# A hybrid attention layer on one core: the first weights on ScalarE's queue, the last product's last step in column halves, and a block of each last row on GpSimd

## The chip, the cores and the metric

The kernel runs on one core of a Trainium2 chip. The metric is the device time of one execution in microseconds (us); the lower the better. A core has five engines, each with its own instruction stream: TensorE (PE in the profile; PEld is its weight load), VectorE (DVE), ScalarE (ACT), GpSimd (POOL) and SyncE (SP). Here SyncE only issues transfers. A transfer can also be issued by ScalarE or GpSimd; the issue then stands in that engine's stream. The engines wait for each other by semaphores. TensorE writes to PSUM, whose banks hold 512 float32 columns on each of 128 partitions; VectorE and ScalarE read PSUM, GpSimd does not here.

## The reference, cut to what matters

One encoder layer over 16 meta tokens and 512 real tokens of width 2048:

```python
hn = rmsnorm(h, pre_norm_g[layer])
proj = jnp.einsum('bld,dc->blc', hn, w_in[layer])
qa, ka, va, ga, qb, kb, vb, gb = jnp.split(proj, SPLIT_POINTS, axis=-1)
ya = gqa_axial_mixer(qa, ka, va, ...) * jax.nn.silu(ga)
yb = diff_attn_mixer(qb, kb, vb, ...) * jax.nn.silu(gb)
y = jnp.einsum('blc,cd->bld', jnp.concatenate([ya, yb], axis=-1), w_out[layer])
h = h + rmsnorm(y, post_norm_g[layer])
return h[:, N_META:, :]
```

For this text two places matter: the first product (`hn` times the first columns of `w_in`) and the very last steps (`y`, its norm over the 2048 columns of each token, the gain, the residual).

## The kernel before, in words

Every float32 operand is split into two parts of a reduced float32 format, a high part (`wh`, `xh`, `t4h`: a copy on ScalarE) and a low part (`wl`, `xl`, `t4l`: the difference, on VectorE), and each product is three matmuls: high times high, low times high, high times low (`three`, and in `product` the three `mm` of `step`).

**The start.** SyncE's queue brings, in program order (`load` pins each transfer behind what was traced on its engine before), the tokens `xs` (one of 16 slices of 128 input columns by 528 tokens each) and the weights `st` (for two slices, 768 columns). ScalarE issues only `gcol`, the gain column, and then runs a small activation `warm`, ahead of which its function table is loaded. `xload(k)` scales a token slice by the gain into `xh[k]` (ScalarE, L191) and `xl[k]` (VectorE, L192). `wload` brings weights and splits them by `wsplit` (L156, L157); the first weights come in two parts of 384 columns, the first for slice 0, the second for slice 1. Meanwhile TensorE runs 16 matmuls on zeros (`heat`, into `hot`). Then the first product runs over the slices k: for each, three groups of columns (a group of keys in two halves of 264 tokens, two groups of 512 tokens), three matmuls each.

The middle (projections, two kinds of attention, the gates) isn't touched.

**The end.** The output projection is made of four blocks of 512 columns and four rows of 128 tokens (`y[t][g]`), by sums of blocks that need fewer products. The last call of `product` makes the last block (g = 2) of rows 0 and 1 (u = 0, 1): its first step i = 0 runs for both rows, then the last three steps first for row 0, followed by `done(0, ...)`, and then for row 1, followed by `done(1, ...)`. Here `done` is `end`. For its row it subtracts the product in PSUM from the block (VectorE, L1173), squares and sums it (ScalarE, L1082), takes the root with the partial sum of the other three blocks, `sspart` (ScalarE, L1162), multiplies by the gain `gpB` (VectorE, L1085), takes the reciprocal (VectorE, L1178), and then for each of the four blocks `row_block` (VectorE, L1167) scales by the row's factor `ry`, adds the residual `xres`, and has SyncE store 128x512 to the output. `order` (the same as `keep_in_program_order`) pins each of these behind the instruction traced before it on its engine. `GS = (0, 3, 1, 2)` is the order of the blocks. Row 0's fourth block is put behind row 1's subtraction. `part` (POOL, L1109 and L1111) makes `sspart` earlier.

What is not pinned is ordered by a scheduler with priorities; `lanes` interleaves the matmuls of attention with the rest by estimated times.

Of the kernel before, what the change touches and what calls it, by code (L numbers as in the profile page):

```python
# [10 lines left out]
F32 = mybir.dt.float32  # L11
F32R = mybir.dt.float32r
F16 = mybir.dt.float16
AF = mybir.ActivationFunctionType
ALU = mybir.AluOpType
AX = mybir.AxisListType

P = 128
DM = 2048
KT = DM // P  # L20
SEQ = 512
NM = 16
NT = SEQ + NM
TT = SEQ // P
HALF = NT // 2
# [16 lines left out]
class Lanes:  # L42
# [13 lines left out]
    def mm(self, out, lhsT, rhs, start, stop, **kw):  # L56
        n = int(np.prod(rhs.shape[1:]))
        us = max(n, 256) / 2370.0
        if rhs.dtype == F32:
            us = 4 * max(n, 128) / 2370.0  # L60
        self._add(self.nc.tensor.matmul(out, lhsT, rhs, start=start, stop=stop, **kw), us)  # L61
# [45 lines left out]
def kernel(ctx: ExitStack, tc: tile.TileContext, xT, xn, xm, w_s, w_t, w_q, w_o,  # L107
                             gpre, gq, gk, lams, gsub, gpost, ident_d, cos_d, sin_d, dist_d, out):
    nc = tc.nc
    lanes = Lanes(tc)  # L110
    mm, transpose = lanes.mm, lanes.transpose
# [4 lines left out]
    wp = ctx.enter_context(tc.tile_pool(name="wp", bufs=3))  # L116
# [12 lines left out]
    def ctile(shape, name, dt=F32, src=None, pool=cst):  # L129
        t = pool.tile(shape, dt, name=name, tag=name, bufs=1)  # L130
        if src is not None:
            load(t, src)
        return t
# [5 lines left out]
    def load(out, in_):  # L139

        tc.keep_in_program_order(nc.sync.dma_start(out=out, in_=in_))


    def wload(src, n=1024, dma=nc.sync.dma_start, parts=1):
        st = wp.tile([P, 1024], F32, name="st", tag="st")
        ws = None
        for i in range(parts):
            c = slice(i * n // parts, (i + 1) * n // parts)
            dma(out=st[:, c], in_=src if parts == 1 else src[:, c])
            ws = wsplit(st, c, ws)  # L150
        return ws

    def wsplit(st, c=slice(0, 1024), ws=None):
        wh, wl = ws or [wp.tile([P, 1024], F32R, name=n, tag=n) for n in ("wh", "wl")]
        with tc.high_priority(rank[0]):
            splits.append((nc.scalar.activation(wh[:, c], st[:, c], AF.Copy),  # L156
                           nc.vector.tensor_tensor(out=wl[:, c], in0=st[:, c],  # L157
                                                   in1=wh[:, c].bitcast(F32), op=ALU.subtract)))
        return wh, wl

    splits = []
# [3 lines left out]
    epst = ctile([P, 1], "epst")  # L165
    nc.vector.memset(epst, EPS)
    warm = ctile([P, 1], "warm")
    nc.scalar.activation(warm, epst, AF.Identity)

    heat = ap.tile([P, 256], F32R, name="heat", tag="pm", bufs=1)  # L170
    nc.vector.memset(heat.bitcast(F32), 0.0)
# [1 line left out]
    hot = pd.tile([P, 512], F32, name="hot", tag="pd")  # L173
    for i in range(16):
        mm(hot[:, :256], heat[:, :P], heat, start=True, stop=True)
    gcol = ctile([P, KT], "gcol")
    nc.scalar.dma_start(out=gcol, in_=gpre)

    def xtile(name, n, dt=F32R):

        return xp.tile([P, 576], dt, name=name, tag=f"x{n}")

    xh, xl = [[xtile(f"x{n}{k}", 2 * k + j)[:, :NT] for k in range(KT)]
              for j, n in enumerate("hl")]
    pad(xp, "xpad", 32)

    def xload(k):
        tag, n = ("p", 4) if k % 6 < 4 else ("tT", 2)
        st = ap.tile([P, NT], F32, name="xs", tag=tag, bufs=n)
        load(st, xT[k])  # L190
        nc.scalar.activation(xh[k], st, AF.Identity, scale=gcol[:, k:k + 1])  # L191
        nc.vector.scalar_tensor_tensor(out=xl[k], in0=st, scalar=gcol[:, k:k + 1],  # L192
                                       in1=xh[k].bitcast(F32), op0=ALU.mult, op1=ALU.subtract)

    KEYS = [(0, HALF), (HALF, NT)]
    REAL = [(NM, NT)]
# [1 line left out]
    def three(ps, wh, wl, k, n0, n1):  # L198
        mm(ps, wh, xh[k][:, n0:n1], start=(k == 0), stop=False)
        mm(ps, wh, xl[k][:, n0:n1], start=False, stop=False)  # L200
        mm(ps, wl, xh[k][:, n0:n1], start=False, stop=(k == KT - 1))
# [40 lines left out]
    start = [KEYS, REAL, REAL]  # L242
    first = [[pd.tile([P, 512], F32, name="pd", tag="pd") for _ in segs] for segs in start]
    for k0 in range(0, KT, 2):
        xload(k0)
        wh, wl = wload(w_s[k0 // 2], 768, load, 2 if k0 == 0 else 1)
        xload(k0 + 1)
        for k in (k0, k0 + 1):
            for i, (segs, pss) in enumerate(zip(start, first)):
                c = slice((i + 3 * (k - k0)) * P, (i + 3 * (k - k0) + 1) * P)  # L250
                for (n0, n1), ps in zip(segs, pss):
                    three(ps[:, :n1 - n0], wh[:, c], wl[:, c], k, n0, n1)
# [22 lines left out]
    for t in (TT, 0, 1, 2, 3):  # L275
        rows = P if t < TT else NM
        src = xn[t * P:(t + 1) * P, :] if t < TT else xm
        for j in range(2 if t < 2 else 4):

            tag, w = ("pl", "pt")[j % 2], 1024  # L280
            if t >= 2:
                tag, w = ("f", "g", "ql")[t - 2], 512
            st = (gp if tag == "g" else ap).tile([P, w], F32, name="xns", tag=tag,
                                                 bufs=2 if t < 2 else 4)[:rows]
            load(st, src[:, j * w:(j + 1) * w])
            acc = ssx[:, t, j:j + 1] if t < TT else ssm[:, j:j + 1]
            if j % 2:
                nc.vector.tensor_tensor_reduce(out=st, in0=st, in1=st, scale=1.0, scalar=0.0,
                                               op0=ALU.mult, op1=ALU.add, accum_out=acc)
            else:  # L290
# [10 lines left out]
                            op0=ALU.mult)  # L301
    for t in range(TT):
        nc.vector.tensor_scalar(out=dg[:, NM + t * P:NM + (t + 1) * P], in0=ident,
                                scalar1=rt[:, t:t + 1], scalar2=None, op0=ALU.mult)
# [11 lines left out]
    def tables():  # L316
        for a in range(2):
# [8 lines left out]
                            op0=ALU.mult)  # L326
# [544 lines left out]
    pss = dense_T(KEYS, [sc[:, 0, :], sc[:, 1, :]], spread)  # L871
# [12 lines left out]
    v = values(pss)  # L884
# [8 lines left out]
    for h in range(NH):  # L893
# [7 lines left out]
        if h + 1 < NH:  # L901
            pss = dense_T(KEYS)
# [5 lines left out]
            v = values(pss)  # L908
# [11 lines left out]
    pss = dense_T(KEYS)  # L920
# [16 lines left out]
    lo_, hi_ = slice(0, NP), slice(NP, SEQ)  # L937
    TTv, SUB, ADD = nc.vector.tensor_tensor, ALU.subtract, ALU.add
# [54 lines left out]
    def product(ops, pss, more=False, beside=None, done=None, ahead=2):  # L993


        def step(u, i, ws):
            for j in range(2):
                bh, bl = ops(i, j, u)
                c = slice(j * 512, (j + 1) * 512)
                wh, wl = ws[j] if isinstance(ws, list) else [w[:, c] for w in ws]  # L1000
                mm(pss[u], bh, wh, start=(i + j == 0 and not more), stop=False,
                   skip_group_check=more)
                mm(pss[u], bl, wh, start=False, stop=False, skip_group_check=more)
                mm(pss[u], bh, wl, start=False, stop=(i + j == 4), skip_group_check=more)
                lanes.poll()

        for i in range(1 if done else 4):
            ws = fetch(ahead)
            for u in range(2):
                step(u, i, ws)  # L1010
            if beside:
                beside(i)
        if done:
            last = [fetch(len(todo) + len(landing)) for _ in range(3)]
            for u in range(2):
                for i in range(3):
                    step(u, 1 + i, last[i])
                done(u, pss[u])
        return pss

    def of_t(tiles):
        return lambda i, j, u: [t[:, j, u * P:(u + 1) * P] for t in tiles[i]]
# [9 lines left out]
    yp = ctx.enter_context(tc.tile_pool(name="yp", bufs=1, reuse_waits="tile"))  # L1032
    pd2 = ctx.enter_context(tc.tile_pool(name="pd2", bufs=4, space=PSUM, reuse_waits="tile"))
    y = [[yp.tile([P, 512], F32, name=f"y{t}{g}", tag=f"y{t}{g}") for g in range(4)]
         for t in range(TT)]
# [3 lines left out]
    t4 = []  # L1039
    ssy = [yp.tile([P, 4], F32, name=f"ssy{t}", tag=f"ssy{t}") for t in range(TT)]  # L1040
    sspart = [yp.tile([P, 1], F32, name=f"ssp{t}", tag=f"ssp{t}") for t in range(TT)]

    def evict(p):

        for pss, t in zip(held[p], (0, 2)):
            for u, ps in enumerate(pss):
                nc.scalar.activation(y[t + u][PAIRS[p][1]], ps, AF.Copy)
# [28 lines left out]
    for j in range(2):  # L1076
        bring_A(j)

    def square(t, g, src):
        jk = yp.tile([P, 512], F32, name="jko", tag="jko")  # L1080
        at = (0, 1, 3, 2)[g]
        return nc.scalar.activation(jk, src, AF.Square, accum_out=ssy[t][:, at:at + 1])  # L1082

    def by_gain(t, g, src=None):
        return TTv(out=y[t][g], in0=y[t][g] if src is None else src,  # L1085
# [2 lines left out]
    xres, places = {}, [(t, g) for t in (2, 3, 0, 1) for g in (0, 3, 1, 2)]  # L1088
# [69 lines left out]
    order = tc.keep_in_program_order  # L1158

    def row_scale(t):  # L1160
        r = ssy[t][:, 3:4]
        order(nc.scalar.activation(r, r, AF.Sqrt, scale=1.0 / DM, bias=sspart[t]))  # L1162
        return r

    def row_block(t, g):
        v = y[t][g]
        order(nc.vector.scalar_tensor_tensor(out=v, in0=v, scalar=ry[t], in1=xres[t, g],  # L1167
                                             op0=ALU.mult, op1=ALU.add))
        load(out[t * P:(t + 1) * P, g * 512:(g + 1) * 512], v)

    def last_block(t, ps):
        v = y[t][2]
        order(TTv(out=v, in0=ps, in1=v, op=SUB))  # L1173
        order(square(t, 2, v))
        ry[t] = row_scale(t)
# [18 lines left out]
    ry, GS = {}, (0, 3, 1, 2)  # L1194
# [11 lines left out]
    product(of_t(t4), third[0], more=True, ahead=4)  # L1206
    third_done(0, third[0])

    def end(u, ps):
        last_block(u, ps)  # L1210

        if u:
            row_block(0, GS[3])
        order(by_gain(u, 2))
        turned(u)
        for g in GS[:4 if u else 3]:
            row_block(u, g)

    product(of_t(t4), third[1], more=True, done=end)


# [57 lines left out]
```

## Time and profile before

| | |
|---|---|
| median of 3 runs | 889.37 us (889.31 to 890.07) |
| the profiled execution | 888.59 us |
| its span, first to last instruction | 886.8 us |
| TensorE busy | 868.8 us, 98% |
| VectorE busy | 631.0 us, 71% |
| ScalarE busy | 497.6 us, 56% |
| GpSimd busy | 126.7 us, 14% |
| TensorE's granted clock, mean | 0.993 |
| bytes moved, mean rate | 185.49 MB, 209 GB/s |

The span is shorter than the time of an execution, which also holds what lies around the instructions. Matmuls are pipelined, so a row's duration is longer than the distance to the next matmul's start. A row of the timeline gives the start, the duration, the engine, the line, the operation, output<-inputs, the shape, how many instructions are merged in the row, and in brackets how long the engine stood idle before and what ended that. VectorE's instructions overlap a little: the next can start some 0.1 us before the end of the one ahead. An engine name with a q (SPq, ACTq) is its queue: the issue of a transfer or a wait.

### The profile page before, as it was taken

The page shows a single profiled execution, that of the slowest core. Times are in us where ns is not written, and L with a number is a line of the kernel's source. Part 1 is how long each engine was busy: PE and PEld are TensorE (multiplying, and loading weights), DVE is VectorE, ACT ScalarE, POOL GpSimd, SP SyncE. Part 2 cuts the span into 40 slices and gives each one's busy share as a digit, 9 for nine tenths or more (in the row PEclk, how much of TensorE's full clock was granted, in tenths as well). Part 3 has the DMA queues.
Part 4 walks back from the last instruction along what each step waited for, and adds up shares of the span by engine and source line. Part 5 has one row for each costly group of instructions (what it writes and reads, how often), then busy time and mean ns, then how long its engine had stood idle before and what let it go on. Part 6 is the DMA issues. An engine that isn't in the chain of part 4 may idle for free. (4 is left out here: it accounts for less than half of the span.)

```text
span 886.8 us, 14070 instructions
## 1 busy us (share of the span) xinstructions
PE 868.8 (98%) x5130; PEld 772.7 (87%) x5130; DVE 631.0 (71%) x1137; ACT 497.6 (56%) x843; POOL 126.7 (14%) x168
## 2 busy tenths in 40 slices
PE   9999999999999999999999999999999999999996
PEld 8999898998989989898998888988878888888884
DVE  7677786766857679585774485788665785876886
ACT  6565574736546475464744444655575566665561
POOL 0100120211111111111120021432111210000020
PEclk9999999999999999999999999999999999999998
DMA  9854969888788978879552334456565669989784
GB/s 336 273 164 140 240 178 279 198 256 215 217 232 193 259 202 227 231 191 237 150 181 73 108 95 158 145 165 184 173 184 183 193 193 321 317 269 312 264 277 155
DMA packets 80677, 185.49 MB, mean 209 GB/s; under 512 B 15136, under 2 KB 38560, under 8 KB 80224
## 3 DMA queue, kind: packets, MB, share of 16 engines
q1 hardware_dynamic: 75856, 167.81, 58.9%
q0 software_dynamic: 4608, 16.78, 11.1%
q8 instruction: 40, 0.66, 0.3%
q14 instruction: 29, 0.24, 0.1%
q10 hardware_dynamic: 144, 0.01, 0.0%
HBM read 158.34 MB, written 59.77 MB: 246 GB/s over the span
## 5 line engine op out<-in xcount | busy, mean ns | idle before, releaser
L61 PE MATMUL pd<-xh,wh 128*128 128x264 f32 (+1 forms) x992 | 326.9, 330 | 0.0
L61 PE MATMUL pd<-xl,wh 128*128 128x264 f32 (+1 forms) x992 | 323.8, 326 | 0.0
L61 PE MATMUL pd<-xh,wl 128*128 128x264 f32 (+1 forms) x992 | 323.4, 326 | 0.0
L156 ACT ACTIVATE wh<-st 128x1024 fp32r<-128x1024 f32 (+2 forms) x159 | 165.4, 1041 | 178.1 <-PE pd L61 65.2
L157 DVE TENSOR_TENSOR wl<-st,wh 128x1024 fp32r<-128x1024 f32 (+2 forms) x159 | 191.1, 1202 | 92.9 <-ACT wh L156 91.7
L61 PEld LDWEIGHTS pd<-xh,wl 128*128 128x128 f32 x992 | 187.0, 189 | 16.1 <-DVE wl L157 0.2
L61 PEld LDWEIGHTS pd<-xh,wh 128*128 128x128 f32 x992 | 187.6, 189 | 12.2 <-ACT wh L156 0.2
L61 PEld LDWEIGHTS pd<-xl,wh 128*128 128x128 f32 x992 | 187.7, 189 | 10.6
L550 ACT ACTIVATE p<-p,mx 128x528 f32<-128x528 f32 x64 | 47.2, 737 | 52.0 <-DVE mx L542 51.8
L468 DVE STREAM_TRANSPOSE pt<-p 128x512 f32<-128x512 f32 x64 | 44.8, 699 | 8.2 <-POOL p L653 7.7
L61 PE MATMUL pd<-wh,xh 128*128 128x512 f32 x128 | 50.4, 394 | 0.0
L61 PE MATMUL pd<-wl,xh 128*128 128x512 f32 x128 | 49.9, 390 | 0.0
L61 PE MATMUL pd<-wh,xl 128*128 128x512 f32 x128 | 49.9, 390 | 0.0
L555 POOL TENSOR_SCALAR p<-p,sm 128x528 f32<-128x528 f32 x32 | 22.7, 708 | 168.2 <-DVE sm L552 167.9
L542 DVE CUSTOM_DVE_ANT_0 p<-sc,dist 128x528 f32<-128x528 f32 x64 | 44.2, 690 | 3.5 <-PE sc L61 2.6
L651 ACT ACTIVATE p<-p,mxA 128x528 f32<-128x528 f32 x32 | 23.5, 736 | 40.1 <-DVE mxA L647 40.0
L833 POOL DMA_DIRECT2D ws<-in_w_o_dram x32 | 26.8, 837 | 117.9 <-DMA ws<-in_w_o_dram 53.3
L653 POOL TENSOR_SCALAR p<-p,smA 128x528 f32<-128x528 f32 x32 | 26.6, 831 | 115.2 <-DVE smA L652 106.4
L352 DVE TENSOR_TENSOR pl<-pl,ph 128x1024 fp32r<-128x1024 f32 x32 | 40.7, 1271 | 0.3
L499 POOL TENSOR_SCALAR pm<-pm 32x256 fp32r<-32x256 f32 x32 | 23.0, 719 | 116.3 <-ACT pm L349 80.4
L647 DVE CUSTOM_DVE_ANT_0 p<-sc,zed 128x528 f32<-128x528 f32 x32 | 22.3, 698 | 21.9 <-PE sc L61 21.7
L61 PE MATMUL sc<-s,q 128*128 128x264 f32 x128 | 34.5, 290 | 2.4 <-DVE mx L542 2.4
(223 smaller groups left out, 1588.6 us busy)
## 6 DMA issues: line engine op xcount, KB each, us to landing
st<-in_w_t_dram SPq DMA_DIRECT2D x82, 512.0 KB, 4.9
turn<-pt SPq DMA_DIRECT2D x32, 544.0 KB, 3.1
pl<-turn SPq DMA_DIRECT2D x128, 128.0 KB, 4.3
ws<-in_w_o_dram POOLq DMA_DIRECT2D x32, 512.0 KB, 7.7
st<-ws SPq DMA_DIRECT2D x32, 512.0 KB, 4.1
st<-in_w_o_dram SPq DMA_DIRECT2D x22, 512.0 KB, 4.4
ws<-in_w_o_dram SPq DMA_DIRECT2D x16, 512.0 KB, 6.1
ws<-ws SPq DMA_DIRECT2D x16, 512.0 KB, 6.0
```

The source lines that it names most:

```text
L61: self._add(self.nc.tensor.matmul(out, lhsT, rhs, start=start, stop=stop, **kw), us)
L156: splits.append((nc.scalar.activation(wh[:, c], st[:, c], AF.Copy), nc.vector.tensor_tensor(out=wl[:, c], in0=st[:, c], in1=wh[:, c].bitca ...
L157: nc.vector.tensor_tensor(out=wl[:, c], in0=st[:, c], in1=wh[:, c].bitcast(F32), op=ALU.subtract)))
L352: return nc.vector.tensor_tensor(out=dst, in0=src, in1=h.bitcast(F32), op=ALU.subtract)
L468: nc.vector.transpose(pt[:, :1024].rearrange("p (m c t q) -> p c m t q", m=4, c=TT, t=2)[:, :, :, j], p[:, NM:].rearrange("p (c m q) -> p ...
L499: nc.gpsimd.tensor_scalar(out=pm[32:64], in0=pm[0:32].bitcast(F32), scalar1=1.0, scalar2=1.0, op0=ALU.mult, op1=ALU.mult)
L542: maxima.append(nc.vector.tensor_tensor_reduce(out=two(p), in0=sc[:, :, :HALF], in1=two(dist[:, w0:w0 + NT]), scale=-0.125 / slope(h), sca ...
L550: nc.scalar.activation(p2[m], p2[m], AF.Exp, scale=-1.0, bias=mx[:, m:m + 1], accum_out=sm[:, m:m + 1])
L555: nc.gpsimd.tensor_scalar(out=p2[0], in0=p2[0], scalar1=sm[:, 0:1], scalar2=1.0, op0=ALU.mult, op1=ALU.mult)
L651: nc.scalar.activation(p, p, AF.Exp, scale=-1.0, bias=mx, accum_out=sm)
L653: nc.gpsimd.tensor_scalar(out=p, in0=p, scalar1=sm, scalar2=1.0, op0=ALU.mult, op1=ALU.mult)
L833: nc.gpsimd.dma_start(out=dst, in_=src, accum_op=ALU.add)
```

## The change

At the start: `gcol` and then the first weights, in two transfers of 384 columns, are issued on ScalarE's queue ahead of `warm`; SyncE's queue no longer carries them. The first token slice is scaled in two parts (tokens 0 to 263, 264 to 527), and between them the first part of the weights is split; all this in a pinned order, and the token scaling of slices 0 to 2 as well.

At the end: for row 1 the last step (i = 2) of the last product is made in two column halves of 256, with `done` called after each. `end` subtracts and squares by halves; the first half's sum of squares goes into `sslast` and is added to `sspart` on VectorE. Of each row the block GS[0] = 0 is scaled and added on POOL by two instructions (`tensor_scalar`, `tensor_tensor`), and its store is issued after the other three. The other three blocks of each row are VectorE's, all directly behind the row's reciprocal; nothing of row 0 is put into row 1's part any more.

```diff
+    gcol = ctile([P, KT], "gcol")
+    first_in_order = tc.keep_in_program_order
+    first_in_order(nc.scalar.dma_start(out=gcol, in_=gpre))
+    st = wp.tile([P, 1024], F32, name="st", tag="st")
+    cs = slice(0, 384), slice(384, 768)
+    for c in cs:
+        first_in_order(nc.scalar.dma_start(out=st[:, c], in_=w_s[0][:, c]))
+    first_in_order(nc.scalar.activation(warm, epst, AF.Identity))
...
-    gcol = ctile([P, KT], "gcol")
-    nc.scalar.dma_start(out=gcol, in_=gpre)
...
-    def xload(k):
+    def xload(k, between=lambda: None):
...
-        nc.scalar.activation(xh[k], st, AF.Identity, scale=gcol[:, k:k + 1])
-        nc.vector.scalar_tensor_tensor(out=xl[k], in0=st, scalar=gcol[:, k:k + 1],
-                                       in1=xh[k].bitcast(F32), op0=ALU.mult, op1=ALU.subtract)
+        for n0, n1 in ((0, HALF), (HALF, NT)) if k == 0 else ((0, NT),):
+            c = slice(n0, n1)
+            hi_ = nc.scalar.activation(xh[k][:, c], st[:, c], AF.Identity,
+                                       scale=gcol[:, k:k + 1])
+            if k < 3:
+                first_in_order(hi_)
+            lo_ = nc.vector.scalar_tensor_tensor(out=xl[k][:, c], in0=st[:, c],
+                                                 scalar=gcol[:, k:k + 1],
+                                                 in1=xh[k][:, c].bitcast(F32), op0=ALU.mult,
+                                                 op1=ALU.subtract)
+            if k < 3:
+                first_in_order(lo_)
+            if n1 < NT:
+                between()
+                for part in splits[-1]:
+                    first_in_order(part)
...
-        xload(k0)
-        wh, wl = wload(w_s[k0 // 2], 768, load, 2 if k0 == 0 else 1)
+        if k0:
+            xload(k0)
+            wh, wl = wload(w_s[k0 // 2], 768, load)
+        else:
+            ws = []
+            xload(0, lambda: ws.append(wsplit(st, cs[0])))
+            wh, wl = wsplit(st, cs[1], ws[0])
+            for part in splits[-1]:
+                first_in_order(part)
...
             for u in range(2):
                 for i in range(3):
-                    step(u, 1 + i, last[i])
-                done(u, pss[u])
+                    if u and i == 2:
+                        for c in (slice(0, 256), slice(256, 512)):
+                            step(u, 1 + i, [[w[:, c] for w in ws] for ws in last[i]],
+                                 pss[u][:, c])
+                            done(u, pss[u], c)
+                    else:
+                        step(u, 1 + i, last[i])
+                if not u:
+                    done(u, pss[u], slice(0, 512))
...
-    def end(u, ps):
-        last_block(u, ps)
-
-        if u:
-            row_block(0, GS[3])
+    def end(u, ps, c):
+        v = y[u][2][:, c]
+        order(TTv(out=v, in0=ps[:, c], in1=v, op=SUB))
+        if c.stop < 512:
+            order(square(u, 2, v, sslast))
+            order(nc.vector.scalar_tensor_tensor(out=sspart[u], in0=sslast, scalar=1.0 / DM,
+                                                 in1=sspart[u], op0=ALU.mult, op1=ALU.add))
+            return
+        order(square(u, 2, v))
+        ry[u] = row_scale(u)
         order(by_gain(u, 2))
         turned(u)
-        for g in GS[:4 if u else 3]:
+
+        v = y[u][GS[0]]
+        order(nc.gpsimd.tensor_scalar(out=v, in0=v, scalar1=ry[u], scalar2=1.0, op0=ALU.mult,
+                                      op1=ALU.mult))
+        order(nc.gpsimd.tensor_tensor(out=v, in0=v, in1=xres[u, GS[0]], op=ALU.add))
+        for g in GS[1:]:
             row_block(u, g)
+        load(out[u * P:(u + 1) * P, GS[0] * 512:(GS[0] + 1) * 512], v)
```

More of the change, by code (lines that the diff above doesn't have):

```diff
@@ L167 @@
     warm = ctile([P, 1], "warm")
-    nc.scalar.activation(warm, epst, AF.Identity)
+    gcol = ctile([P, KT], "gcol")
[6 more added lines that the diff above has]
+    first_in_order(nc.scalar.activation(warm, epst, AF.Identity))
     heat = ap.tile([P, 256], F32R, name="heat", tag="pm", bufs=1)
@@ L993, in product, with step @@
     def product(ops, pss, more=False, beside=None, done=None, ahead=2):
-        def step(u, i, ws):
+        def step(u, i, ws, ps=None):
+            ps = pss[u] if ps is None else ps
             for j in range(2):
@@ L1000, in step @@
                 wh, wl = ws[j] if isinstance(ws, list) else [w[:, c] for w in ws]
-                mm(pss[u], bh, wh, start=(i + j == 0 and not more), stop=False,
+                mm(ps, bh, wh, start=(i + j == 0 and not more), stop=False,
                    skip_group_check=more)
-                mm(pss[u], bl, wh, start=False, stop=False, skip_group_check=more)
-                mm(pss[u], bh, wl, start=False, stop=(i + j == 4), skip_group_check=more)
+                mm(ps, bl, wh, start=False, stop=False, skip_group_check=more)
+                mm(ps, bh, wl, start=False, stop=(i + j == 4), skip_group_check=more)
                 lanes.poll()
@@ L1041 @@
     sspart = [yp.tile([P, 1], F32, name=f"ssp{t}", tag=f"ssp{t}") for t in range(TT)]
+    sslast = yp.tile([P, 1], F32, name="ssl", tag="ssl")
     def evict(p):
@@ L1077, with square @@
         bring_A(j)
-    def square(t, g, src):
+    def square(t, g, src, to=None):
         jk = yp.tile([P, 512], F32, name="jko", tag="jko")
         at = (0, 1, 3, 2)[g]
-        return nc.scalar.activation(jk, src, AF.Square, accum_out=ssy[t][:, at:at + 1])
+        return nc.scalar.activation(jk[:, :src.shape[-1]], src, AF.Square,
+                                    accum_out=ssy[t][:, at:at + 1] if to is None else to)
     def by_gain(t, g, src=None):
```

## The prediction

> **What bounds the kernel now.** I read the page's head first, then the busy time by stage, then the timeline of both ends.
>
> ```profile
> span 886.8 us, 14070 instructions
> PE 868.8 (98%) x5130; PEld 772.7 (87%) x5130; DVE 631.0 (71%) x1137; ACT 497.6 (56%) x843; POOL 126.7 (14%) x168
> ```
>
> ```profile
> 874.00:887.00 13.00, 4.12 (x19) 3.07 (x17) 8.30 (x14) 2.03 (x6) 0.00 (x0) 0.77 0.42 161
> ```
>
> TensorE (PE) is busy in all but 18.0 us of the span; of these 8.7 lie in the last stage (13.00 - 4.12, less the 0.2 behind the span's end), where POOL does nothing. Both parts of the change are at the ends: the start can win only until the matmuls are dense, the end only in what follows the last matmul. The profiled execution took 888.59 us, 1.79 beyond its span and 0.78 under the median of 889.37; the sum is a difference and is added to the median. About 0.2% (1.78 us) is what can be told from no change.
>
> **The start.** TensorE, then ScalarE, VectorE and SyncE:
>
> ```profile
> 4.58 0.41 PE L61 MATMUL hot<-heat 128*128 128x256 f32 x1
> 4.90 0.59 PE L61 MATMUL pd<-xh,wh 128*128 128x264 f32 x1
> 5.29 0.59 PE L61 MATMUL pd<-xl,wh 128*128 128x264 f32 x1
> 5.76 0.59 PE L61 MATMUL pd<-xh,wl 128*128 128x264 f32 x1
> ...
> 6.80 0.63 PE L61 MATMUL pd<-xh,wh 128*128 128x512 f32 x1
> 7.23 0.44 PE L61 MATMUL pd<-xl,wh 128*128 128x512 f32 x1
> 7.51 0.40 PE L61 MATMUL pd<-xh,wl 128*128 128x512 f32 x1
> ```
>
> ```profile
> 1.17 1.28 ACT L168 ACT_TABLE_LOAD   x1 [1.17 <-PEq L1267]
> ...
> 3.69 0.74 ACT L191 ACTIVATE xh<-xs,gcol 128x528 fp32r<-128x528 f32 x1 [1.03 <-DMA gcol<-in_gpre_dram]
> 4.34 0.92 ACT L156 ACTIVATE wh<-st 128x384 fp32r<-128x384 f32 x2
> ```
>
> ```profile
> 4.47 0.77 DVE L192 SCALAR_TENSOR_TENSOR xl<-xs,gcol,xh 128x528 fp32r<-128x528 f32 x1 [2.85 <-ACT xh L191]
> 5.15 1.02 DVE L157 TENSOR_TENSOR wl<-st,wh 128x384 fp32r<-128x384 f32 x2
> ```
>
> ```profile
> 1.18 0.89 SPq L141 DMA_DIRECT2D st<-in_w_s_dram  x2
> ```
>
> The heating matmuls end at about 4.70, so the first real one (4.90) gains 0.20 at most; the next two waited for xl (ends 5.24) and wl. The gain column that xh waits for is still issued first on ScalarE's queue, so xh starts near 3.69 as now. ScalarE then issues two weight transfers of about 0.45 (0.89 for two on SyncE's queue) ahead of its table load: 1.17 + 0.90 + 1.28 + 0.20 for the small activation = 3.55, still under 3.69. These 0.14 us are the cover. SyncE's queue is relieved of 0.89, and the second token tile comes that much sooner; no matmul waited for it. Half of xh takes about 0.45, the first weight part 0.46 (0.92 for two): both are ready near 4.65, xl's half near 4.6, wl's part near 5.2. The matmul now at 6.80 then comes after three starts spaced by about 0.2 (4.70, 4.92, 5.30) and three more at about 6.26, 0.54 earlier.
>
> These matmuls run at half rate: 512 columns took 0.43 from 6.80 to 7.23 and 0.28 from 7.23 to 7.51. If the change of rate keeps its time, work done 0.54 earlier at half rate is worth 0.27; if it moves with the work, 0.54. The Trainium skill (TensorE: Matmul & The Clock Gate, Part 1) says the rate is raised by a free-running activity window, not by a count of matmuls; by that rule the gain would be the 0.27 and the sum 0.1 higher than mine. I take 0.40 between the two. If the weights or the gain column land late in the new traffic, it is nothing. **Start: -0.40 (0 to -0.54).** The waits of later stages are as before, so I let it through to the end.
>
> **The end.** TensorE's last matmul, VectorE, ScalarE, then the output issues:
>
> ```profile
> 877.73 0.39 PE L61 MATMUL po<-wl,t4h 128*128 128x512 f32 x1
> ```
>
> ```profile
> 876.42 2.08 DVE L1167 SCALAR_TENSOR_TENSOR y<-y,ssy,xr 128x512 f32<-128x512 f32 x3
> 878.42 0.69 DVE L1173 TENSOR_TENSOR y<-po,y 128x512 f32<-128x512 f32 x1
> 879.02 0.74 DVE L1167 SCALAR_TENSOR_TENSOR y<-y,ssy,xr 128x512 f32<-128x512 f32 x1
> 879.89 0.69 DVE L1085 TENSOR_TENSOR y<-y,gpB 128x512 f32<-128x512 f32 x1
> 880.50 0.16 DVE L1178 RECIPROCAL ssy<-ssy 128x1 f32<-128x1 f32 x1
> 880.69 2.74 DVE L1167 SCALAR_TENSOR_TENSOR y<-y,ssy,xr 128x512 f32<-128x512 f32 x4
> ```
>
> ```profile
> 879.13 0.63 ACT L1082 ACTIVATE jko<-y 128x512 f32<-128x512 f32 x1 [3.16 <-DVE y L1173]
> ```
>
> ```profile
> 882.80 0.99 SPq L141 DMA_DIRECT2D out_dram<-y  x2
> ```
>
> The last matmul ends at 878.12, but VectorE is still on row 0's three blocks until its 878.42: the subtraction is bound by VectorE, not by TensorE. Row 0's fourth block (879.02) lies in the shade of the square. So an earlier first column half is worth nothing while VectorE is busy, and POOL taking a block of row 0 saves nothing: VectorE still does three there. What is saved is one of four blocks of row 1.
>
> *POOL's price* is what its block does to VectorE. Rows from the attention stage, where POOL scales 128x528 beside VectorE:
>
> ```profile
> L653 POOL TENSOR_SCALAR p<-p,smA x32: 707/711/2212, 533.4 to 710.9; 128x528 f32<-128x528 f32 x32
> ```
>
> ```profile
> 599.75 1.24 POOL L653 TENSOR_SCALAR p<-p,smA 128x528 f32<-128x528 f32 x1 [1.32 <-DVE smA L652]
> ```
>
> ```profile
> 599.82 0.69 DVE L698 TENSOR_TENSOR kn<-kn,t 128x512 f32<-128x512 f32 x1
> 600.42 0.71 DVE L682 SCALAR_TENSOR_TENSOR qn<-qn,ssh,gqB 128x128 f32<-128x128 f32 x1
> ```
>
> ```profile
> L682 DVE SCALAR_TENSOR_TENSOR qn<-qn,ssh,gqB x32: 333/344/716, 508.2 to 601.3; 128x128 f32<-128x128 f32 x32
> ```
>
> ```profile
> 590.34 1.32 POOL L653 TENSOR_SCALAR p<-p,smA 128x528 f32<-128x528 f32 x1 [2.31 <-DVE smA L652]
> ```
>
> ```profile
> 590.34 0.41 DVE L692 SCALAR_TENSOR_TENSOR t<-kn,sinT 128x256 f32<-128x256 f32 x1
> 590.68 0.41 DVE L694 TENSOR_TENSOR t<-kn,sinT 128x256 f32<-128x256 f32 x1
> ```
>
> At 599.75 POOL took 1.24 instead of 0.71: it stood while VectorE read two SBUF operands, got in as the next VectorE instruction with a per-row scalar began, and that one took 0.71 instead of 0.34. So they exclude each other, and the one-input operation costs VectorE 0.37, or 0.36 at 512 columns. A row block is just such an instruction: two SBUF operands and a per-row scalar. At 590.34 POOL waited out both VectorE instructions (end 591.09) and ran afterwards. POOL's second operation, an add of two tiles, has no row of this size: between 0.36 (as with one input) and 0.72 (each element read twice); between ends a factor of two apart no row is nearer, so I take 0.54. As POOL's own duration, two reads give 0.7 to 1.3; the Trainium skill (GPSIMD Engine Reference, section 3.1) has 4497 ns for an add at 2048 columns, which would be an estimated 1.12 here and leave the sum as it is.
>
> *Half sizes.*
>
> ```profile
> L343 DVE TENSOR_TENSOR vf<-pd,rB 128x264 f32<-128x264 f32 x18 | 7.1, 413 | 0.0
> ```
>
> ```profile
> 8.55 0.85 ACT L156 ACTIVATE wh<-st 128x768 fp32r<-128x768 f32 x1 [0.65 <-DMA st<-in_w_s_dram]
> ```
>
> ```profile
> 859.14 1.05 ACT L156 ACTIVATE wh<-st 128x1024 fp32r<-128x1024 f32 x1
> ```
>
> ```profile
> 8.80 0.28 PE L61 MATMUL pd<-xh,wh 128*128 128x264 f32 x1
> 8.92 0.28 PE L61 MATMUL pd<-xl,wh 128*128 128x264 f32 x1
> ```
>
> A half subtraction is 0.42. 256 columns less are 0.20 less on ScalarE, so square to gain product falls from 0.76 (879.13 to 879.89) to 0.56. Six half matmuls are 5 x 0.12 + 0.28 = 0.88.
>
> Whether the second half's matmuls wait until the first half of the same bank has been read, no row shows: nowhere here is a bank written in one part and read in another. Not waiting, they are long done, and the second subtraction waits for the first half's square and the small add (0.42 + 0.02 + 0.56 + 0.08 = 1.08 after the first starts). Waiting, it comes at 0.42 + 0.06 + 0.88 + 0.03 = 1.39. I take 1.39, because every bank in the trace is written whole and then read. The Trainium skill (PSUM — Partial Sum Buffer, PSUM bank collisions raise a hardware error) says semaphores must guard PSUM by bank, not by address; by that rule it is the 1.39, and TensorE stands between the halves.
>
> The sum, against 883.46, the last output issue (882.80 plus 0.66):
> 1. Row 0's three blocks with POOL among them: 0.36 + 0.54 = **+0.90**; the first subtraction starts at 879.32.
> 2. Subtraction to gain product: now 879.89 - 878.42 = 1.47; then 1.39 + 0.42 + 0.02 + 0.56 = 2.39: **+0.92** (+0.61 without the wait).
> 3. Gain product, reciprocal to first block (879.89 to 880.69): unchanged, 0.80.
> 4. Row 1's blocks: 2.08 + 0.90 = 2.98 against 2.74: **+0.24**.
> 5. POOL's block is issued on SyncE's queue behind block 2, 0.33 later, and moves beside it; until now they were 0.66 apart: **+0.60** (0.33 to 0.66).
>
> End: +2.66; with the start **+2.3**, so 889.37 + 2.3 = **891.7**. All low ends together (two times 0.18 for POOL, 0.31, 0.27, 0.14 at the start) give 890.5, the high ones 892.5.
>
> **The rivals.**
> - *POOL starves* as at 590.34. VectorE's row blocks stay undisturbed; POOL's two operations on row 0 run from 878.42 to 880.06, the small add (two SBUF inputs) waits for them, the second subtraction comes at 880.06, the first block of row 1 at 881.86, the last ends 883.94, and POOL only then does its own: 0.57 + 0.09 + 0.98 to 885.5. +2.1 at the end, +1.7 in all: 891.1. Against it: two instructions with a per-row scalar let POOL in.
> - *Not slower: POOL works beside VectorE at no price.* For it: 707 ns is the minimum and 711 the median of 32, and this pair ran side by side:
>
> ```profile
> 608.49 0.71 POOL L653 TENSOR_SCALAR p<-p,smA 128x528 f32<-128x528 f32 x1 [5.43 <-DVE smA L652]
> ```
>
> ```profile
> 608.23 0.67 DVE L352 TENSOR_TENSOR kl<-tr,kh 128x512 fp32r<-128x512 f32 x1
> ```
>
> But that VectorE instruction has one of its operands (tr) in PSUM; a row block has both in SBUF. At no price, terms 1 and 4 are 0 and 2.08 - 2.74 = -0.66: 0.92 - 0.66 + 0.60 - 0.40 = +0.5, 889.9; also without the wait between halves 889.6. It decides if POOL's two operations fit in three blocks' 2.08 (0.69 + 0.1 + 0.98 do).
> - *Faster by over 0.2%* needs 1.8 us; the largest start (0.54), a saved block (0.66) and no cost of the halves come to 1.2. Only a better order in the middle could add the rest.
>
> **How the numbers follow.** The forecast 0.55, starving 0.13, no price 0.26, all else 0.06. Slower by over 0.2% is above 891.15: most of the forecast (0.44), half of the starving case, a little of the rest: 0.53. Faster 0.04, same 0.43. The forecast's own range is 890.5 to 892.5; for 8 in 10 the range takes in the no-price case: 889.4 to 892.6.
>
> **What would show it.** In the changed profile row blocks at the end of over 1.0 us beside POOL, POOL's first operation well over 0.7, the first half subtraction after 879, a gap on TensorE of over 1 us before the last six matmuls, the last output issued near 886, and the first real matmul at 4.7. It is wrong if row blocks stay at 0.75 beside a running POOL (then 889.9 or less), or if the weight transfers delay xh past 3.9.

## The result, and the profile after

The changed kernel takes 894.03 us (median of 9 runs, 890.53 to 895.71), the kernel before 888.72 (median of 9, 885.08 to 890.50). The ratio is 1.0054, 95% interval 1.0038 to 1.0069: slower by 4.8 us (3.4 to 6.1), where 2.3 were forecast. Slower was right, the size was not, and the time lies outside the range.

The executions of either kernel are spread over some 5 us, and in the changed kernel the time follows the mean granted TensorE clock: 890.53 us at 0.995, 895.71 at 0.990. In the profile of before (span 886.8) this clock falls to 0.50 for 3.4 us twice, near 598 and 666 us; in the profile after (span 889.5) it never does between the ends, and the stretch between them is 2.5 us shorter. So the spans differ by only 2.7, and the two ends are compared by themselves. "Slice 2 begins" is the start of the first matmul on token slice 2; "end stage" goes from the start of row 0's subtraction to the end of the span.

| us | before | after | difference | forecast |
|---|---|---|---|---|
| first real matmul | 4.90 | 5.59 | +0.69 | -0.20 |
| slice 2 begins | 10.53 | 11.85 | +1.32 | -0.40 |
| end stage | 12.7 | 16.6 | +3.9 | +2.66 |

The two ends together are +5.2. Each row compares one execution with one. The end stage is alike wherever the same end was profiled (12.7 or 16.6); the start is not, as the experiments show.

The start after, ScalarE's timeline, then TensorE's, then the transfers with their median time from issue to landing in us, and last the weights' transfers of before:

```profile
1.16 0.94 ACTq L175 DMA_DIRECT2D st<-in_w_s_dram  x2
2.13 1.28 ACT L176 ACT_TABLE_LOAD   x1 [2.13 <-issue]
3.42 0.20 ACT L176 ACTIVATE warm<-epst 128x1 f32<-128x1 f32 x1
3.80 0.52 ACT L200 ACTIVATE xh<-xs,gcol 128x264 fp32r<-128x264 f32 x1 [0.17 <-DMA gcol<-in_gpre_dram]
5.01 0.52 ACT L156 ACTIVATE wh<-st 128x384 fp32r<-128x384 f32 x1 [0.70 <-DMA st<-in_w_s_dram]
```

```profile
5.59 0.59 PE L61 MATMUL pd<-xh,wh 128*128 128x264 f32 x1 [0.60 <-ACT wh L156]
...
8.51 0.63 PE L61 MATMUL pd<-xh,wh 128*128 128x512 f32 x1
8.93 0.63 PE L61 MATMUL pd<-xl,wh 128*128 128x512 f32 x1
9.36 0.55 PE L61 MATMUL pd<-xh,wl 128*128 128x512 f32 x1
9.74 0.28 PE L61 MATMUL pd<-xh,wh 128*128 128x264 f32 x1
```

```profile
xs<-in_xT_dram SPq DMA_DIRECT2D x3, 264.0 KB, 3.6
st<-in_w_s_dram ACTq DMA_DIRECT2D x2, 192.0 KB, 4.2
```

```profile
st<-in_w_s_dram SPq DMA_DIRECT2D x2, 192.0 KB, 2.9
```

The table load fits as worked out (small activation from 3.42), and xh starts at 3.80. But now ScalarE stands 0.70 for the weights, whose first part lands 3.8 us after its issue instead of 2.8 (each transfer by itself). And 512 columns still take 0.42 at 8.51: the full rate comes at about 9.4, two microseconds later than in the profile of before.

The end after: VectorE, POOL, TensorE between the halves.

```profile
872.88 0.69 DVE L1249 TENSOR_TENSOR y<-po,y 128x512 f32<-128x512 f32 x1 [2.44 <-PE po L61]
...
875.23 3.52 DVE L1205 SCALAR_TENSOR_TENSOR y<-y,ssy,xr 128x512 f32<-128x512 f32 x3
878.67 0.41 DVE L1249 TENSOR_TENSOR y<-po,y 128x256 f32<-128x256 f32 x1
879.73 0.16 DVE L1252 SCALAR_TENSOR_TENSOR ssp<-ssl,ssp 128x1 f32<-128x1 f32 x1 [0.65 <-ACT jko L1119]
880.15 0.42 DVE L1249 TENSOR_TENSOR y<-po,y 128x256 f32<-128x256 f32 x1 [0.26 <-PE po L61]
881.21 0.69 DVE L1123 TENSOR_TENSOR y<-y,gpB 128x512 f32<-128x512 f32 x1 [0.63 <-ACT jko L1119]
...
882.01 3.52 DVE L1205 SCALAR_TENSOR_TENSOR y<-y,ssy,xr 128x512 f32<-128x512 f32 x3
```

```profile
875.37 1.17 POOL L1261 TENSOR_SCALAR y<-y,ssy 128x512 f32<-128x512 f32 x1 [4.14 <-DVE ssy L1216]
876.62 1.57 POOL L1263 TENSOR_TENSOR y<-y,xr 128x512 f32<-128x512 f32 x1
```

```profile
879.13 0.39 PE L61 MATMUL po<-wh,t4h 128*128 128x256 f32 x1 [2.86 <-DVE y L1249]
```

Three row blocks take 3.52 instead of 2.08. One by one (narrow windows of the same timeline) they start at 875.23, 875.90 and 877.00 and take 0.75, 1.18 and 1.75:

```profile
875.23 0.75 DVE L1205 SCALAR_TENSOR_TENSOR y<-y,ssy,xr 128x512 f32<-128x512 f32 x1
```

```profile
875.90 1.18 DVE L1205 SCALAR_TENSOR_TENSOR y<-y,ssy,xr 128x512 f32<-128x512 f32 x1
```

```profile
877.00 1.75 DVE L1205 SCALAR_TENSOR_TENSOR y<-y,ssy,xr 128x512 f32<-128x512 f32 x1
```

The first is as before, the second 0.43 longer (POOL's one-input operation got in), the third 1.00 longer (its two-input one). TensorE idles 2.86 between the column halves, until VectorE has read the first.

### The profile page after: what moved, and what is told of

Read it like the earlier page. It is cut to its first block, busy times and chain, and to the rows that moved or that the text cites. A ratio compares the mean times of both kernels' runs of the same rounds, so it can differ in the third digit from the quotient of the medians.

```text
span 889.5 us, 14097 instructions
## 1 busy us (share of the span) xinstructions
PE 866.9 (97%) x5136; PEld 771.1 (87%) x5136; DVE 631.9 (71%) x1138; ACT 496.9 (56%) x846; POOL 125.8 (14%) x172
## 5 line engine op out<-in xcount | busy, mean ns | idle before, releaser
L526 POOL TENSOR_SCALAR pm<-pm 32x256 fp32r<-32x256 f32 x32 | 21.1, 660 | 111.1 <-ACT pm L376 75.7
```

## The experiments

**The two ends apart.** The first run has the diff's start and the old end, the second the old start and the diff's end.

> The start of the change alone, the end as before. Theory (the first weights land later on ScalarE's queue because SyncE's next token and weight transfers now run beside them, TensorE idles about 0.9 us before its first real matmul, and the full rate comes some 2 us later): the first real matmul at about 5.6 instead of 4.9, slice 1's matmuls begin at about 9.7 instead of 8.4, and the end stage (row 0's subtraction to the end of the span) stays at 12.7; time +1.0 to +1.6 us. Rival (the start is worth what was forecast, and the trace of the changed kernel was one unlucky execution): slice 1 begins at about 8.0 and the time is 0.4 us lower.

> The end of the change alone, the start as before. Theory (the end's price is POOL's block excluding VectorE plus the wait between the halves): first real matmul at 4.9, end stage 16.6 us instead of 12.7, time +3.9 us. Rival (the end costs the forecast 2.7 and the remaining loss came from the start and from the middle): end stage about 15.4, time +2.7.

Start alone: ratio 1.0017 (1.0003 to 1.0031), that is +1.5 us (0.3 to 2.8). The weights' first part landed 4.4 us after issue, the first real matmul came at 6.18, slice 1 at 10.04, slice 2 at 12.59. End alone: ratio 1.0056 (1.0038 to 1.0075), +5.0 us; end stage 16.6 us, row blocks 3.52 again, first real matmul at 4.83. The interval of the end alone (3.4 to 6.7 us) holds 3.9, not 2.7. So both ends lose. The two alone add up to 6.5, the whole is +4.8 and the two ends of its profile are +5.2; within these intervals nothing is left for the middle, but an effect there of a microsecond isn't excluded.

**Why the start loses: queue, parts, or rate.** In one run the two parts and the pinned order stay, but the weights go back to SyncE's queue; in another TensorE heats longer.

```diff
-    for c in cs:
-        first_in_order(nc.scalar.dma_start(out=st[:, c], in_=w_s[0][:, c]))
...
         load(st, xT[k])
+        if k == 0:
+            for c in cs:
+                load(first_w[:, c], w_s[0][:, c])
```

> The tokens in two parts and the pinned order, but the first weights on SyncE's queue behind the first tokens, as before; the end as before. Theory (the queue is at fault, not the two parts): no idle ahead of the first real matmul, which comes at 4.7; slice 1 begins at 8.0 to 8.3; time 0.1 to 0.4 us lower, which is within noise. Rival (the two parts or the pinned order cost it): first real matmul later than 5.2, slice 1 after 9.

Ratio 0.9997 (0.9984 to 1.0010); first real matmul at 4.79, slice 2 at 10.25 instead of 10.53. A gap opens inside slice 1 (one matmul at 7.52, the next at 8.18), since its tokens are late, so the gain is 0.28. That is less than the spread of the old start itself: in the six profiles that have it (the kernel before and five of the runs here) slice 2 begins at 10.01 to 11.35, and in four of them slice 1 stops for its tokens too. The first real matmul tells the starts apart more clearly: 4.83 to 5.07 in these six, 5.59 to 6.18 in the three with the weights on ScalarE's queue and nothing held. The parts are harmless; the queue is at fault.

> As the run with the start alone, but 20 heating matmuls instead of 16, so that TensorE works until about 5.6 and does not idle ahead of its first real matmul. Theory (the idle 0.9 us keeps the rate at half for longer): full rate again at about 7.3 to 7.5, slice 1 begins at about 8.6 to 8.9, so a good half of the start's loss is gone although the first real matmul still comes at about 5.6. Rival (the rate's change comes at another moment in each execution, whatever TensorE does): full rate at about 9.5 as in the changed kernel, slice 1 at about 9.7.

The change is `range(20)` for `range(16)` at the heating matmuls. The first real matmul came only at 5.99, yet full rate was there at 7.4, slice 1 began at 8.90 and slice 2 at 11.01, 1.6 earlier than with the start alone. Ratio 1.0011 (0.9996 to 1.0026): the time can't tell it from the start alone, the two timelines differ. TensorE in the start alone, then with longer heating:

```profile
6.18 0.39 PE L61 MATMUL pd<-xh,wh 128*128 128x264 f32 x1 [1.51 <-ACT wh L156]
...
7.53 0.59 PE L61 MATMUL pd<-xh,wh 128*128 128x512 f32 x1
7.91 0.63 PE L61 MATMUL pd<-xl,wh 128*128 128x512 f32 x1
8.34 0.63 PE L61 MATMUL pd<-xh,wl 128*128 128x512 f32 x1
```

```profile
7.54 0.40 PE L61 MATMUL pd<-xh,wh 128*128 128x512 f32 x1
7.77 0.39 PE L61 MATMUL pd<-xl,wh 128*128 128x512 f32 x1
8.00 0.39 PE L61 MATMUL pd<-xh,wl 128*128 128x512 f32 x1
```

In the start alone a matmul of 512 columns at 7.91 takes 0.43 to the next, with longer heating 0.23 at 7.54: the idle 1.51 us ahead of 6.18 was followed by a stretch at half rate that lasted until 10.93. Both are single executions, and the moment at which the rate rises isn't the same in every one: in the ten profiles without idle time ahead of the first real matmul it lies between 5.5 and 7.5 us. That idle time brings or prolongs the half rate is supported, not proved.

The granted clock also shows that the half rates of the start alone and of the changed kernel aren't the same. In the start alone the matmuls behind the gap ran at full rate, and the clock then fell to 0.50, from about 7.6 to 11.0. In the changed kernel it reads 1.00 all the way, and the full rate simply came late, at about 9.4. So the run with the start alone doesn't by itself explain the second 0.63 of the changed kernel's 1.32; the first 0.69 is the late first matmul.

**Why the weights land late.**

```diff
         load(st, xT[k])        # for k == 1, in front of it:
+        if k == 1:
+            nc.gpsimd.tensor_copy(out=st[:, :1], in_=first_w[:, :1])
```

> As the run with the start alone, but SyncE's second token transfer, and so all behind it on SyncE's queue, is held until the first weights part has landed (a one-column copy on POOL from the weights into the token tile, which the transfer then overwrites). Theory (the weights come late because SyncE's next transfers share the transfer engines with them): the weights land about 3 us after their issue as before, instead of 4.2 to 4.9, the first real matmul comes at 4.7 to 4.9, and slice 1 waits for its tokens instead. Rival (ScalarE's queue itself is slower): the weights still land more than 4 us after their issue and the first real matmul comes after 5.5.

```profile
st<-in_w_s_dram ACTq DMA_DIRECT2D x2, 192.0 KB, 3.1
xs<-in_xT_dram SPq DMA_DIRECT2D x1, 264.0 KB, 2.8
```

With SyncE's further transfers held, the weights land 3.1 us after issue instead of 4.2 to 4.9 (the median of the two parts), their first part 2.8 instead of 3.8 to 4.4. The first 264-column part of the tokens is followed at once by the weights' split (3.73 and 4.15 on ScalarE), and the first real matmul comes at 4.79. So ScalarE's queue is not slow by itself; SyncE's next transfers, in flight beside it, hold the weights up. This is one execution, but the first part of the weights separates without overlap: 2.8 to 2.9 us in all eight profiles with the weights on SyncE's queue. (The second part doesn't: 2.9 to 5.3 there, 4.5 to 5.3 on ScalarE's.) Slice 2 begins at 10.84, as slice 1 now waits for its tokens, and slice 2 stops once more for its weights.

**The end's parts.** One run keeps POOL's blocks and makes the last step whole; one keeps the halves and gives all blocks to VectorE.

> The end of the change with POOL's blocks, but the last step whole; the start as before. Theory (the parts add up): end stage 12.7 + 1.44 + 0.78 + 0.60 = 15.5 us, 1.1 less than with the halves; time +2.8 us against before. Rival (the halves hide something and pay for themselves): end stage 16.6 or more.

> The end of the change with the column halves, but all four blocks of each row on VectorE, row 0's four ahead of row 1's subtraction; the start as before. Theory: every row block stays at 0.75, the first half subtraction comes one block (0.66) later than before, subtraction to gain product takes 2.5 instead of 1.5: end stage 12.7 + 0.7 + 1.1 = 14.4 us, time +1.7 us. Rival (POOL's part is harmless and the halves are the price): end stage above 16.

Row 0's blocks on VectorE, first with POOL and whole, then with halves and without POOL:

```profile
874.91 3.52 DVE L1170 SCALAR_TENSOR_TENSOR y<-y,ssy,xr 128x512 f32<-128x512 f32 x3
```

```profile
878.80 2.74 DVE L1178 SCALAR_TENSOR_TENSOR y<-y,ssy,xr 128x512 f32<-128x512 f32 x4
```

POOL without halves: end stage 15.5 (872.57 to 888.1), blocks 3.52 and 3.51; ratio 1.0037 (1.0020 to 1.0055), +3.3. Halves without POOL: end stage 14.4 (876.46 to 890.9), four blocks in 2.74; ratio 1.0021 (1.0007 to 1.0036), +1.9. Both as the sums say. Each part loses by itself: POOL's blocks 2.8 (with the 0.60 of their later store), the halves 1.1, to which 0.7 comes with row 0's fourth block no longer in the shade of row 1's square.

**What in POOL's part costs.** First VectorE's second operand comes from PSUM (these blocks leave out the residual), then POOL does only one operation (its block leaves out the residual).

```diff
-        for g in GS[1:]:
-            row_block(u, g)
+        for g in GS[1:]:
+            b = y[u][g]
+            order(nc.vector.scalar_tensor_tensor(out=b, in0=b, scalar=ry[u], in1=third[0][u],
+                                                 op0=ALU.mult, op1=ALU.add))
+            load(out[u * P:(u + 1) * P, g * 512:(g + 1) * 512], b)
```

> The end of the change, the start as before; VectorE's row blocks take their second operand from a finished bank of PSUM instead of the residual in SBUF (so these blocks leave the residual out). Theory (POOL and VectorE exclude each other only while VectorE reads two operands in SBUF): the row blocks are back at about 0.75 beside POOL, POOL's first operation takes about 0.7 and its second 1.0 to 1.2, end stage about 13.7 us. Rival (POOL slows any VectorE work beside it, or the per-row scalar is the cause): blocks of 1.2 and 1.75 us as in the changed kernel, end stage 16.6.

```profile
L1239 DVE SCALAR_TENSOR_TENSOR y<-y,ssy,po x6: 739/742/748, 875.0 to 881.6; 128x512 f32<-128x512 f32 x6
```

```profile
875.11 0.69 POOL L1234 TENSOR_SCALAR y<-y,ssy 128x512 f32<-128x512 f32 x1 [2.74 <-DVE ssy L1189]
875.89 1.26 POOL L1236 TENSOR_TENSOR y<-y,xr 128x512 f32<-128x512 f32 x1
```

The columns of the first line are minimum, median and maximum in ns. Six blocks at 739 to 748 ns beside a running POOL, and POOL itself at 0.69 and 1.26 instead of 1.17 and 1.57; end stage 13.7 (872.63 to 886.3). The per-row scalar is still there, so it is not enough by itself: the cost needs both of VectorE's operands in SBUF.

> The end of the change, the start as before; POOL only scales its block and the residual isn't added to it (this leaves out the residual of one block per row). Theory (POOL's first operation costs one VectorE block about 0.4 and its second, with two inputs, costs another 1.0): of three row blocks one is at about 1.17 and two at 0.75, end stage 16.6 - 2 x 1.0 = 14.6 us. Rival (the cost is one of POOL running at all, not of what it reads): more than one block is stretched, or one by over 0.6; end stage above 15.

```profile
877.68 2.51 DVE L1178 SCALAR_TENSOR_TENSOR y<-y,ssy,xr 128x512 f32<-128x512 f32 x3
```

Three blocks in 2.51, 0.43 above 2.08; end stage 14.6 (875.34 to 889.9). So the one-input operation costs 0.43 per row and the two-input one 1.0.

**A version meant to beat both.**

```diff
+        y[u][2] = early[0][:, u * 512:(u + 1) * 512]
+        order(TTv(out=y[u][2], in0=v, in1=gpB[:, 1024:1536], op=ALU.mult))
+        if u:
+            row_block(0, GS[3])
         turned(u)
```

> A version meant to beat both: the start with the tokens in two parts and the weights on SyncE's queue; the last step whole and all blocks on VectorE as before, but the gain product of the last block writes another tile, so that it need not wait until ScalarE has squared the block, and is issued right behind the subtraction. Theory: row 0's blocks start 0.2 earlier, VectorE is then just free when the last matmul ends (0.2 to 0.3 won), and row 1's reciprocal comes 0.2 earlier: end stage 12.3 instead of 12.7; with the start 0.6 us in all, within what the runs can tell. Rival (the reciprocal waits for ScalarE's root anyway and nothing is won): end stage 12.6 to 12.8.

```profile
880.69 0.69 DVE L1246 TENSOR_TENSOR wr<-y,gpB 128x512 f32<-128x512 f32 x1
881.30 0.74 DVE L1198 SCALAR_TENSOR_TENSOR wr<-wr,ssy,xr 128x512 f32<-128x512 f32 x1
881.97 0.15 DVE L1209 RECIPROCAL ssy<-ssy 128x1 f32<-128x1 f32 x1
```

End stage 12.45 (875.85 to 888.3) instead of 12.7. The gain product starts 0.71 behind the subtraction (879.98), where the row block of before started 0.60 behind, and row 0's fourth block now keeps VectorE until 881.97, so the reciprocal waits for VectorE and a part of the 0.4 is lost. Ratio 0.9990 (0.9977 to 1.0003): not told apart from the kernel before, but by the two ratios (1.0054 / 0.9990) 0.6% faster than the changed one, about 0.4 to 0.8% from both intervals.

## Why the prediction was right or wrong

- *Start, sign wrong.* The step that failed is "both are ready near 4.65", and with it the bound "if the weights or the gain column land late in the new traffic, it is nothing". I counted the second token tile's earlier issue as free, since no matmul waited for it, and kept the weights' landing as it was. SyncE's earlier transfers held the weights up: the first part landed 3.8 us after its issue instead of 2.8, and 2.8 again when they were held. The first real matmul came 0.69 later instead of 0.20 earlier, and I had put the cost of late weights at zero. The +1.32 at slice 2, where -0.40 was forecast, compares two executions, and its second half is a rate that rose late, at a moment that varies anyway; in the time the start alone costs 0.3 to 2.8 us. The sign that I had named, xh past 3.9, didn't show: xh started at 3.80, and it was the weights behind it that were late.
- *Two smaller errors at the start.* The heating matmuls follow each other at 0.21, so the first real one could start at 4.79, as it does in three runs, and not at 4.70. And "the waits of later stages are as before" doesn't hold: with the weights on SyncE's queue and the tokens in two parts, slice 1 stopped for its tokens, and the gain of slice 0 was mostly lost there.
- *Term 1 (+0.90) and term 4 (+0.24), mechanism right, size wrong:* 1.44 and 0.78. POOL got in where a row block began, as at 599.75, but its add held VectorE for 1.00, not 0.54; the first operation 0.43, not 0.36. The upper end, 0.72, came from counting bytes read, and was itself too low.
- *Term 2 (+0.92):* 2.54 instead of 2.39 from subtraction to gain product, +1.07. The wait between the halves is there (2.86 on TensorE); the first matmul behind it takes 0.23 to the next instead of 0.12.
- *Term 3 (0)* and *term 5 (+0.60):* term 3 is 0.80 as before; from the last row block's end (885.53) to the span's end 3.97 instead of 3.37, +0.60.
- *Sum of the end:* 1.44 + 1.07 + 0.78 + 0.60 = 3.89. The terms divide one stretch of time, so they must add up; that its parts also cost this much separately is what the two runs with 15.5 and 14.4 us show.
- *Rivals.* POOL starved in no run of the changed end; POOL at no price fell with the blocks of 1.18 and 1.75. The shading of row 0's fourth block, which the change gives up, was named and is worth 0.7 where POOL does not take a block (the run with halves alone).
- *Range.* It had the start's gain as its worst case at zero and the add at 0.72; the two misses (1.7 at the start, 1.2 at the end) went the same way. Slower was right by the end alone, where the mechanism held.
- *The bank rule and the add's duration.* TensorE stood 2.86 us between halves of one bank, until VectorE had read the first half. The rule by bank in the Trainium skill (PSUM — Partial Sum Buffer, PSUM bank collisions raise a hardware error) agrees with that wait. POOL's add took 1.26 beside VectorE instructions with one operand in PSUM, 1.57 beside those with both in SBUF. The Trainium skill (GPSIMD Engine Reference, section 3.1) gave an estimated 1.12 for it.

## What to carry to other kernels

A transfer that nobody waits for isn't free to be moved ahead: on a second queue it runs beside the one that is waited for, and in both profiles here with an early gap on TensorE a longer stretch at half rate came behind it. An engine that takes work off another must be priced by what it does to the other's instructions in the same microseconds: here two operations of POOL cost VectorE 1.44 us to save it one of 0.67. And before a last step is cut in two, look which engine the first half would wait for: VectorE was busy, and the second half's matmuls waited until the first half of their bank had been read.

## What the runs showed of the hardware that I had not expected

- POOL's add of two 128x512 tiles in SBUF held back a VectorE instruction with two SBUF operands for 1.00 us and itself took 1.57; with one of VectorE's operands in PSUM VectorE wasn't slowed (742 ns), and the add took 1.26.
- In the start alone 1.51 us without matmuls were followed by full rate (0.12 between matmuls of 264 columns at 7.41), and then by 3.4 us at half rate (7.53 to 10.93), in which the granted clock reads 0.50. The half rate of the first microseconds is another thing: the granted clock reads 1.00 there, while 512 columns take 0.42.
- The granted clock goes to 0.50 for 3.4 us at a time. TensorE waits some 1.5 us near 595 and 3.0 us near 664 in the kernel before, and as long in the changed one; behind these waits the clock fell for 3.4 us each in the profile of before and not at all in the one after, and in the other runs' profiles for 0 to 10.2 us in sum. So the same idle time can be followed by a slow stretch or not. By estimate each stretch lowers the mean clock by 0.002 (1.7 of 890 us), and the changed kernel's means from 0.990 to 0.995 lie two or three of them apart; its other executions have no profile that shows them.
- The first of two transfers of 192 KB landed 2.8 to 2.9 us after its issue in a queue's turn (eight profiles), and in 3.8 to 4.4 when the other queue had three of 264 KB and more in flight beside it.
